# Transposing the softmax of a group of queries one group later

## The chip, the cores and the metric

The kernel runs on one core of one Trainium2 chip. The metric is the device time of one execution in microseconds (us). Before the change it is 2257.52 us in the median of three runs (2251.76 to 2259.87).

The engines are named as in the profile: PE is TensorE (matrix products, transposes), PEld its loading of weights, DVE is VectorE, ACT is ScalarE, POOL is GpSimd, SP is the engine that issues nearly all DMAs.

## The reference

One layer mixes three branches over 2048 positions of width 1024: a gated short convolution, a Fourier mix, and attention over a neighbourhood. What matters here is the attention. Positions form a grid of 32 rows by 64 columns. A block of 16 query columns in one row looks at 8 rows of keys in a window of 32 columns, with a learned bias and a mask, and also at 256 context keys. One softmax goes over both:

```python
s_loc = jnp.einsum('bnqhd,binchd->bhnqic', qr, kb).astype(jnp.float32) * scale + bias
s_loc = jnp.where(mask, s_loc, NEG_INF)
s_ctx = jnp.einsum('bnqhd,bkhd->bhnqk', qr, k_ctx).astype(jnp.float32) * scale
sc = jnp.concatenate([s_loc.reshape(b, h, n_cb, Q_BLOCK_W, n_loc), s_ctx], axis=-1)
p = jax.nn.softmax(sc, axis=-1).astype(v.dtype)
```

The weights p are then applied to the values of the window and of the context. Before this come a normalization and one wide projection of the input to all branches; after it a projection per branch, sigmoid gates, an output projection and a last normalization.

## The kernel before

The wide projection is done in pairs of output tiles, with a scheme of seven products for each pair. A product is twelve matmuls of 128x512 (lines 310 to 312) into one of three banks (mm). After each of its seven products a pair calls a background hook.

In the second half of the projection the hook (line 1141) advances a generator, `both`, by 2.7 steps a call on the average. It yields first the steps of `attention`, then those of `fourier`, then some preparations of the tail. So the program text is a sequence of products with a few attention steps after each. The framework then orders the instructions of each engine when the program is built: the place in the text is the priority, and an instruction whose operands or buffers it holds to be late lets others go ahead. On the chip each engine works off its list in that order.

Attention goes over 32 units (4 pairs of heads, 4 blocks of columns, 2 heads of the pair), and in each unit over 4 groups of 128 queries, 128 groups in all. Each group has these steps:

- scores (`scores`): the bias is loaded (line 823). Four matmuls give the context scores sx and the window scores sl (lines 883 to 886). VectorE takes the maxima and writes the biased scores into a tile P (lines 890, 891), ScalarE exponentiates (lines 893, 894), VectorE adds up, inverts and normalizes P (lines 895 to 897). P has three buffers, sl one bank, sx two.
- turn (`do_turn`, `turn`): P is transposed in five or six pieces (line 931), three at a time into one bank (tr); each batch is copied to a tile PT (line 941), the first by VectorE, the second by ScalarE. PT has four buffers, two for each group. The first turn of a block of columns also loads its values vt (line 912), which have one buffer.
- weigh: after every second turn the transposed weights of two groups are multiplied with the values (line 953, bank po), the result is copied by ScalarE (line 954), and after two such steps stored (line 957).

With the scores of the last group of a unit, `prepare_qk` loads queries and keys of the next one. The keys are split into KH by ScalarE (line 131) and KL by GpSimd (line 132); KH and KL have one buffer each, T, the scaled queries, two.

A turn isn't taken right after its scores: it is put into a list, `turns`, and taken from it one group later, after that group's scores. Likewise the weigh that a turn makes due goes into a list, `weighs`, and is taken after the next scores. So in a unit the steps are: scores and turn for the first and third group, and scores, weigh and turn for the second and fourth.

Of the kernel before, what the change touches and what calls it, by code (L numbers as in the profile page):

```python
# [59 lines left out]
def emit(tc, I, out, dbg=None):  # L60
# [776 lines left out]
    def attention():  # L837
# [4 lines left out]
        def keys_ctx(pr):  # L842
            r = []
            for hd in range(2):
                raw = at.tile([128, 512], F32, tag="raw", name="rawc", bufs=3)
                dup_load(raw[:, :CT], kcd[pr][hd * 64 : hd * 64 + 64, :])
                a = at.tile([128, CT], F32R, tag="kch", name="kch", bufs=2)
                b_ = at.tile([128, CT], F32R, tag="kcl", name="kcl", bufs=2)
                split(a, b_, raw[:, :CT], nc.scalar, nc.gpsimd)
                r.append((a, b_))  # L850
            return r
# [19 lines left out]
        def scores(head, ct, g, qk, kc, bt):  # L871

            T, KH, KL = qk
            w = KW[ct]
            n = G_NR[g] * w
            if g != 2:
                bt = at.tile([128, 480], F32, tag="bt", name="bt", bufs=2)
                bias_load(head, CTYPE[ct], g, n, w, bt)
            sl = pat.tile([128, 512], F32, tag="sl", name="sl")
            sx = pat.tile([128, CT], F32, tag="sx", name="sx", bufs=2)  # L880
            tq = T[:, g * 128 : g * 128 + 128]
            ks = slice(G_R0[g] * w, G_R0[g] * w + n)
            nc.tensor.matmul(sx, tq, kc[0], start=True, stop=False)
            nc.tensor.matmul(sx, tq, kc[1], start=False, stop=True)
            nc.tensor.matmul(sl[:, :n], tq, KH[:, ks], start=True, stop=False)
            nc.tensor.matmul(sl[:, :n], tq, KL[:, ks], start=False, stop=True)
            P = at.tile([128, CT + 480], F32, tag="P", name="P", bufs=3)
            Pl = P[:, CT : CT + n]
            sm = smt()
            nc.vector.tensor_reduce(sm[:, 0:1], sx, AX.X, ALU.max)  # L890
            nc.vector.tensor_tensor_reduce(Pl, sl[:, :n], bt[:, :n], 1.0, sm[:, 0:1], ALU.add, ALU.max, accum_out=sm[:, 1:2])
            nc.vector.tensor_scalar(sm[:, 2:3], sm[:, 1:2], -1.0, None, ALU.mult)
            nc.scalar.activation(P[:, :CT], sx, AF.Exp, bias=sm[:, 2:3], accum_out=sm[:, 3:4])
            nc.scalar.activation(Pl, Pl, AF.Exp, bias=sm[:, 2:3], accum_out=sm[:, 4:5])
            nc.vector.tensor_scalar(sm[:, 5:6], sm[:, 3:4], sm[:, 4:5], 2.0, ALU.add, ALU.mult)
            nc.vector.reciprocal(sm[:, 6:7], sm[:, 5:6])
            nc.vector.tensor_scalar(P[:, : CT + n], P[:, : CT + n], sm[:, 6:7], None, ALU.mult)
            return P, bt
# [5 lines left out]
        def values(pr, ct):  # L904
            vt = at.tile([128, 9, 128], F32, tag="vt", name="vt")
            c0, w = KCS[ct], KW[ct]
            pieces = ((0, 0, 4, 8),) if w == 32 else ((1, 4, 5, 3), (4, 12, 5, 4), (0, 0, 4, 1), (8, 20, 2, 1))
            for first, row, rows, cnt in pieces:
                for r in range(rows):
                    base = vd[pr][(row + r) * 64 + c0 : (row + r) * 64 + c0 + w, :]  # L910
                    src = AP(tensor=base.tensor, offset=base.offset, ap=[[128, w], [rows * 64 * 128, cnt], [1, 128]])
                    load(vt[r * w : r * w + w, first : first + cnt, :], src)
            return vt

        def turn(head, ct, g, P, vt):

            p0 = head % 2 * 64
            w = KW[ct]
            n = G_NR[g] * w
            ch = [(P[:, x * 128 : x * 128 + 128], 128, vc[x][:, head * 64 : head * 64 + 64]) for x in range(2)]  # L920
            at_ = 0
            for piece_, rows in (MID if w == 32 else EDGE)[g]:
                e = min(at_ + 128, n)
                ch.append((P[:, CT + at_ : CT + e], e - at_, vt[: rows * w, piece_, p0 : p0 + 64]))
                at_ += rows * w
            lst = []
            for c0 in range(0, len(ch), 3):
                grp = ch[c0 : c0 + 3]
                pt = pat.tile([128, 512], F32, tag="tr", name="tr")
                for x, (src, w_, _) in enumerate(grp):  # L930
                    nc.tensor.transpose(pt[:w_, x * 128 : x * 128 + 128], src, ident)  # L931
                PT = at.tile([128, 384], F32, tag="PT", name="PT", bufs=PTB)
                eng = nc.vector if c0 == 0 else nc.scalar
                x = 0
                while x < len(grp):
                    y = x
                    while y < len(grp) and grp[y][1] == grp[x][1]:
                        y += 1
                    w_ = grp[x][1]
                    d_, s_ = PT[:w_, x * 128 : y * 128], pt[:w_, x * 128 : y * 128]  # L940
                    eng.copy(d_, s_) if eng is nc.scalar else eng.tensor_copy(d_, s_)  # L941
                    x = y
                for x, (_, _, v_) in enumerate(grp):
                    lst.append((v_, PT[: v_.shape[0], x * 128 : x * 128 + 128]))
            return lst

        def weigh(pr, ct, hd, gp, pts, ost):
            po = pat.tile([128, 128], F32, tag="po", name="po")
            for x in range(max(len(l) for l in pts)):
                for z in range(2):  # L950
                    if x < len(pts[z]):
                        v_, p_ = pts[z][x]
                        nc.tensor.matmul(po[z * 64 : z * 64 + 64, :], v_, p_, start=x == 0, stop=x == len(pts[z]) - 1)
            nc.scalar.copy(ost[:, gp, :], po)
            if gp == 1:
                for z in range(2):
                    store(od[pr][hd * 64 : hd * 64 + 64, z::2, ct, :], ost[z * 64 : z * 64 + 64])

        turns, weighs = [], []
        V = {}  # L960

        def do_turn(pr, ct, hd, g, P):
            if (pr, ct) not in V:
                V[pr, ct] = values(pr, ct)
            lst = turn(2 * pr + hd, ct, g, P, V[pr, ct])
            if g % 2 == 0:
                V["half"] = lst
                if g == 0:
                    V["ost"] = at.tile([128, 2, 128], F32, tag="ost", name="ost")
            else:  # L970
                weighs.append((pr, ct, hd, g // 2, [V["half"], lst], V["ost"]))
# [4 lines left out]
        for i, (pr, ct, hd) in enumerate(groups):  # L976
            bt = None
            for g in range(4):
                P, bt = scores(2 * pr + hd, ct, g, qk, kc[hd], bt)
                if g == 3 and i + 1 < len(groups):  # L980
                    if groups[i + 1][0] != pr:
                        kc = keys_ctx(groups[i + 1][0])
                    qk = prepare_qk(*groups[i + 1])
                yield
                if weighs:
                    weigh(*weighs.pop())
                    yield
                if turns:
                    do_turn(*turns.pop())
                    yield  # L990
                turns.append((pr, ct, hd, g, P))
        do_turn(*turns.pop())
        yield
        weigh(*weighs.pop())
        yield
        et.close()

    def fourier():
# [133 lines left out]
    def both():  # L1132
        yield from attention()
        vcs.close()
        yield from fourier()
        yield from tail_pools()
# [229 lines left out]
```

## Time and profile before

| | us |
|---|---|
| median of three runs | 2257.52 |
| lowest and highest | 2251.76, 2259.87 |
| the profiled execution | 2256.13 |
| its span, from first to last instruction | 2254.4 |
| PE busy | 2132.9 |
| DVE busy | 1547.0 |
| ACT busy | 887.1 |
| POOL busy | 1011.5 |

The profile is of one execution. An engine is busy while one of its instructions runs; the matmuls are pipelined, so that a busy PE needn't be a PE at its peak. Idle time is put down to what ended it. Attention lies between about 915 and 1570 us of the span. Lines are those of the kernel; lines 131, 132 and 310 to 312 belong to helpers that many places use, and the names of the tiles tell these apart.

### The profile page before, as it was taken

What the parts mean: (1) busy time and instruction counts of PE and PEld (TensorE: products, weight loads), DVE (VectorE), ACT (ScalarE), POOL (GpSimd) and SP (SyncE); (2) the same over time, 40 slices, a digit from 0 to 9 for tenths busy, and PEclk for the clock granted to TensorE, in tenths of its full rate; (3) what the DMA queues carried; (4) which work ended last, traced back from release to release, by engine and by line L of the source; (5) the groups of instructions that cost most, each with busy time, mean ns of one, the idle gap of its engine ahead of it and who ended that gap; (6) DMA issues with size and microseconds to landing.
All of it is one profiled execution on the core that took longest, in us unless ns stands there. A gap on an engine that the chain in (4) does not pass through costs nothing. (4 is left out here: it accounts for less than half of the span.)

```text
span 2254.4 us, 32033 instructions
## 1 busy us (share of the span) xinstructions
PE 2132.9 (95%) x10588; PEld 1686.6 (75%) x10588; DVE 1547.0 (69%) x2731; ACT 887.1 (39%) x2011; POOL 1011.5 (45%) x761
## 2 busy tenths in 40 slices
PE   6899989999999899999999999999999898999998
PEld 4678768888788687777777777777757677878777
DVE  6864685565665665778787788786736868787773
ACT  3443222334544442454555555554213332222121
POOL 2753467654464654444444334343415243434341
PEclk8999999999999899999999999999999999999999
DMA  6244644233233344343444444453466676666561
GB/s 255 80 136 117 225 174 168 94 108 117 94 101 111 101 142 131 109 126 107 142 127 127 139 148 127 141 149 127 154 211 218 212 223 214 192 206 191 173 190 67
DMA packets 198863, 336.78 MB, mean 149 GB/s; under 512 B 22249, under 2 KB 89129, under 8 KB 197546
## 3 DMA queue, kind: packets, MB, share of 16 engines
q1 hardware_dynamic: 198554, 334.47, 46.8%
q8 instruction: 84, 1.38, 0.3%
q14 instruction: 81, 0.66, 0.1%
q10 hardware_dynamic: 144, 0.26, 0.0%
HBM read 248.27 MB, written 86.38 MB: 148 GB/s over the span
## 5 line engine op out<-in xcount | busy, mean ns | idle before, releaser
L131 ACT CAST wh<-wr 128x512 fp32r<-128x512 f32 x384 | 237.7, 620 | 479.1 <-PE mm L311 388.1
L132 DVE TENSOR_TENSOR wl<-wr,wh 128x512 fp32r<-128x512 f32 x256 | 244.7, 957 | 37.0 <-ACT wh L131 36.8
L132 POOL TENSOR_TENSOR wl<-wr,wh 128x512 fp32r<-128x512 f32 x128 | 173.7, 1360 | 212.8 <-ACT wh L131 191.0
L337 POOL TENSOR_TENSOR ws<-wr 128x512 f32<-128x512 f32 x62 | 89.0, 1435 | 309.0 <-DMA wr<-w_in 255.3
L395 DVE SCALAR_TENSOR_TENSOR st<-mm,bin,tp 128x512 f32<-128x512 f32 x158 | 118.0, 747 | 143.0 <-PE mm L312 136.0
L132 POOL TENSOR_TENSOR wbl<-wr,wbh 128x512 fp32r<-128x512 f32 x96 | 130.9, 1367 | 163.0 <-ACT wbh L131 160.4
L126 PE MATMUL mm<-yh,wbh 128*128 128x512 f32 x384 | 153.5, 400 | 17.8 <-DVE tg L1238 10.4
L128 PE MATMUL mm<-yh,wbl 128*128 128x512 f32 x384 | 152.8, 398 | 2.3 <-POOL wbl L132 2.3
L127 PE MATMUL mm<-yl,wbh 128*128 128x512 f32 x384 | 151.8, 396 | 0.3 <-DVE yl L132 0.3
L931 PE MATMUL tr<-ident,P 128*128 128x128 f32 (+3 forms) x672 | 120.4, 280 | 19.1 <-DVE PT L941 7.9
L132 POOL TENSOR_TENSOR wl<-ws,wh 128x512 fp32r<-128x512 f32 x62 | 83.7, 1350 | 112.5 <-ACT wh L131 94.8
L931 PEld LDWEIGHTS tr<-ident,P 128*128 128x128 f32 (+3 forms) x672 | 78.9, 139 | 68.4 <-DVE PT L941 25.4
L355 POOL TENSOR_TENSOR wr<-wr 128x512 f32<-128x512 f32 x64 | 87.9, 1373 | 93.7 <-DVE wl L132 58.8
L450 DVE TENSOR_TENSOR st<-mm,tp 128x512 f32<-128x512 f32 x96 | 65.9, 686 | 87.2 <-PE mm L312 84.4
L310 PE MATMUL mm<-B11h,wh 128*128 128x512 f32 x256 | 104.5, 408 | 14.0 <-DVE tp L353 7.4
L131 ACT CAST wbh<-wr 128x512 fp32r<-128x512 f32 x96 | 59.2, 620 | 127.6 <-PE mm L127 61.0
L126 PE MATMUL po<-wo,mh 128*128 128x512 f32 x256 | 101.2, 395 | 7.8 <-DVE xn L1261 7.7
L310 PE MATMUL mm<-T4h,wh 128*128 128x512 f32 x256 | 103.1, 403 | 4.5 <-DVE tp L345 4.5
L311 PE MATMUL mm<-B11l,wh 128*128 128x512 f32 x256 | 103.0, 402 | 4.2 <-DVE B11l L132 4.2
L339 POOL TENSOR_TENSOR wr<-ws,wr 128x512 f32<-128x512 f32 x62 | 84.3, 1360 | 49.6 <-DVE wl L132 36.3
L310 PE MATMUL mm<-B21h,wh 128*128 128x512 f32 x256 | 102.6, 401 | 3.6 <-DVE st L450 2.8
L310 PE MATMUL mm<-T2h,wh 128*128 128x512 f32 x256 | 102.8, 402 | 1.4 <-ACT T2h L131 1.4
(319 smaller groups left out, 6293.3 us busy)
## 6 DMA issues: line engine op xcount, KB each, us to landing
wr<-w_in SPq DMA_DIRECT2D x136, 512.0 KB
gd<-st SPq DMA_DIRECT2D x96, 256.0 KB
wr<-w_br SPq DMA_DIRECT2D x96, 256.0 KB
tg<-gd SPq DMA_DIRECT2D x96, 256.0 KB
tab<-dft SPq DMA_DIRECT2D x40, 256.0 KB
wa<-w_ada SPq DMA_DIRECT2D x32, 256.0 KB
rawq<-qd SPq DMA_DIRECT2D x64, 128.0 KB
rawk<-kd SPq DMA_DIRECT2D x64, 128.0 KB
```

The lines of the kernel that those rows point to most:

```text
L126: nc.tensor.matmul(ps, ah, bh, start=first, stop=False)
L127: nc.tensor.matmul(ps, ah, bl, start=False, stop=False)
L128: nc.tensor.matmul(ps, al, bh, start=False, stop=last)
L131: heng.copy(hi, src) if heng is nc.scalar else heng.tensor_copy(hi, src)
L132: return leng.tensor_tensor(lo, src, hi.bitcast(F32), ALU.subtract)
L310: nc.tensor.matmul(ps, w[0][:, s], oh, start=first and k == 0, stop=False)
L311: nc.tensor.matmul(ps, w[0][:, s], ol, start=False, stop=False)
L337: ptt(t1, a21, a22, ALU.add)
L339: ptt(a11, t1, a11, ALU.subtract)
L355: ptt(a12, a12, a11, ALU.subtract)
L395: stt(dst, ps, bc(m), add, ALU.add, ALU.add)
L931: nc.tensor.transpose(pt[:w_, x * 128 : x * 128 + 128], src, ident)
```

## The change

The list `turns` now holds two groups: after the scores of a group the turn of the group two before it is taken, the oldest first, where it was the turn of the group before. The weigh still follows the turn that makes it due by one group, so it moves with it. At the end two turns are left, and each is followed by a weigh if one is due.

```diff
                 if weighs:
                     weigh(*weighs.pop())
                     yield
-                if turns:
-                    do_turn(*turns.pop())
+                if len(turns) > 1:
+                    do_turn(*turns.pop(0))
                     yield
                 turns.append((pr, ct, hd, g, P))
-        do_turn(*turns.pop())
-        yield
-        weigh(*weighs.pop())
-        yield
+        while turns:
+            do_turn(*turns.pop(0))
+            yield
+            if weighs:
+                weigh(*weighs.pop())
+                yield
         et.close()
```

Buffers, instructions and their number stay as they are. In a unit the steps become: scores, weigh and turn for the first and third group, scores and turn for the second and fourth.

## Rows read from the trace of the kernel before

**Rows 1.** The page: busy us, share of the span and instructions of each engine.

```profile
PE 2132.9 (95%) x10588; PEld 1686.6 (75%) x10588; DVE 1547.0 (69%) x2731; ACT 887.1 (39%) x2011; POOL 1011.5 (45%) x761
```

**Rows 2.** Busy time by stretch: length, five engines, granted clock, DMA share, GB/s.

```profile
915.00:1570.00 655.00, 633.42 (x3998) 484.93 (x3998) 517.67 (x1300) 349.78 (x1069) 270.79 (x207) 1.00 0.44 129
1570.00:2254.00 684.00, 641.75 (x2751) 501.22 (x2749) 460.23 (x662) 181.03 (x322) 255.92 (x198) 0.98 0.58 189
```

**Rows 3.** Waits of PE, 915 to 1570 us: us in total, times, longest.

```profile
PE tr L931 <- DVE PT L941: 7.9, 19, 1.2
PE tr L931 <- DVE P L897: 7.9, 10, 2.3
PE sl L886 <- POOL KL L132: 2.4, 2, 1.3
PE tr L931 <- DVE sm L896: 1.1, 1, 1.1
PE tr L931 <- DVE sm L892: 1.1, 2, 0.9
PE tr L931 <- DVE sm L895: 0.4, 1, 0.4
```

**Rows 4.** In order of time, one change of unit: start, duration, engine, line, operation.

```profile
1110.79 0.36 PE L883 MATMUL sx<-kch,T 128*128 128x256 f32 x1
...
1113.27 2.51 POOL L132 TENSOR_TENSOR KL<-rawk,KH 128x512 fp32r<-128x512 f32 x2
...
1117.41 0.50 DVE L897 TENSOR_SCALAR P<-P,sm 128x544 f32<-128x544 f32 x1
...
1117.47 0.37 PE L883 MATMUL sx<-kch,T 128*128 128x256 f32 x1
...
1121.46 0.49 PE L931 MATMUL tr<-ident,P 128*128 128x128 f32 x3
...
1121.71 0.36 PE L883 MATMUL sx<-kch,T 128*128 128x256 f32 x1
```

**Rows 5.** Waits of PE's weight loads, 915 to 1570 us.

```profile
PEld tr L931 <- DVE PT L941: 25.4, 66, 1.6
...
PEld tr L931 <- DVE P L897: 6.3, 5, 2.8
```

**Rows 6.** In order of time: last and first scores around two changes of unit.

```profile
929.67 0.28 PE L883 MATMUL sx<-kch,T 128*128 128x256 f32 x1
...
937.06 0.28 PE L883 MATMUL sx<-kch,T 128*128 128x256 f32 x1
...
1535.78 0.28 PE L883 MATMUL sx<-kch,T 128*128 128x256 f32 x1
...
1540.06 0.36 PE L883 MATMUL sx<-kch,T 128*128 128x256 f32 x1
```

**Rows 7.** The chain in order of time: one weigh (start, us, what).

```profile
1546.45 1.75 PE po L953 x20
```

**Rows 8.** In order of time: VectorE's writes of P beside transposes, two places.

```profile
950.14 0.52 DVE L891 CUSTOM_DVE_ANT_0 P<-sl,bt,sm 128x288 f32<-128x288 f32 x1 [0.20 <-PE sl L886]
...
950.40 0.38 PE L931 MATMUL tr<-ident,P 128*128 128x128 f32 x2
...
1532.36 0.44 PE L931 MATMUL tr<-ident,P 128*128 128x128 f32 x2
...
1532.78 0.59 DVE L891 CUSTOM_DVE_ANT_0 P<-sl,bt,sm 128x360 f32<-128x360 f32 x1
```

**Rows 9.** Waits of SP's queue, 915 to 1570 us.

```profile
SPq L912 <- PE po L953: 17.5, 10, 2.6
```

**Rows 10.** In order of time, the end of attention.

```profile
1561.98 0.47 PE L310 MATMUL mm<-B11h,wh 128*128 128x512 f32 x1
...
1563.30 0.54 PE L953 MATMUL po<-PT,vc 128*64 128x128 f32 x5
```

## The prediction

> **What bounds the kernel now.** I read the page's busy times first [rows 1]: TensorE is busy 95% of the span, the next engine, VectorE, 69%. Then the same by stretch [rows 2]: attention runs as background work from about 915 to 1570 us. In these 655.0 us TensorE is busy 633.4 us, so it idles 21.6 us; VectorE is busy 517.7 us, so it idles 137.3 us. The granted clock there is 1.00, so no clock is to be won or lost. A change to the order of the steps of attention that adds and removes no instruction can change only such idle time. Then the waits of TensorE in this stretch [rows 3]. The reader is to see that nearly all of them stand before the transposes of line 931, and that they are of two kinds: the one bank for transposed tiles is still being copied out (PT, 7.9 us in 19 waits), or the softmax is not yet normalized (P, 7.9 us in 10 waits; sm, which is VectorE still at the small steps of a softmax, 1.1 + 1.1 + 0.4 us in 4). The second kind is 10.5 us together. No matmul of the projection products (mm) is in the list.
>
> Last, single places in order of time. One shows where the planner really puts things [rows 4]. The scores of one group start at 1110.79, its softmax is normalized from 1117.41 to 1117.91, and its transposes start at 1121.46. Between them stand the scores of the next group (1117.47); those of the one after it start at 1121.71. So a softmax takes 7.1 us from its scores to its end, longer than the 6.7 and 4.2 us from one group's scores to the next, and the transposes, one group late in the program, run on the chip almost two groups late already, just ahead of the scores of the second group after.
>
> **The change, part by part.** I write S(n) for the scores and softmax of group n, T(n) for its transposes and their copies, W for the values of two groups. Counts stay: 128 S, 128 T, 64 W, 320 steps, so what follows attention starts at the same place between the products, and only waits are to be summed.
>
> *T(n) moves from between S(n+1) and S(n+2) to between S(n+2) and S(n+3).* What goes is the wait for the softmax, 10.5 us [rows 3]. On the chip T(n) already ran next to S(n+2), so I expect it to move behind S(n+2): which makes it later by the four matmuls of these scores, and by more wherever a product lies between. The waits were 0.75 us in the mean (10.5 us over 14) and 2.3 us at most, so I let all but parts of the longest go and take 9 us; below stands 0 (the planner lets the new place slide until it is as tight again), above the 10.5 us, and with the weight loads that waited for P while a matmul still drained (6.3 us in 5 [rows 5]) 16.8 us. Here the Trainium skill speaks ("Perfetto Trace Analysis", section "Identifying the Most-Contended Engine"): matmul busy time flatters a pipelined engine, and the busy share of weight loads shows the headroom better. The trace agrees that the two differ: in this stretch weight loads are busy 484.9 of 655.0 us, 74%, against 97%. Read by that rule the gain would be the 16.8 us and not 9; I keep the matmul rows, since a weight load that waits while a matmul drains costs nothing until the array is empty.
>
> *What is late next: the copy out of the bank.* A turn's second transposes need VectorE's copy of the first and the one bank. That wait (7.9 us) stays as it is, since the copies and their bank are untouched. Bounds: all 7.9 us could go if VectorE's order happens to become kinder; it could double. I take 0, no reason for either sign.
>
> *W moves by one group too, and leaves the place behind the loading of new keys.* Before, the steps between the last scores of a unit S(3) and the first of the next unit S(0') were W and T; after, T alone. S(0') needs KL, and KH and KL have one buffer each: S(3) must have read them, then ScalarE casts, then GpSimd subtracts. At the place shown GpSimd ends at 1115.78, 5.0 us after S(3) started [rows 4]. From S(3) to S(0') it is 7.39 us at the first of 31 such places and 4.28 us at the last [rows 6], in the mean over the 31 about 6.4 us. Without W, whose 20 matmuls take 1.75 us [rows 7], S(0') comes due at or before the end of KL nearly everywhere. The planner then puts products, W or T ahead of it, so the price is only where GpSimd is later than planned. Today that happens 2 times of 31, 2.4 us together [rows 3]. Ends: 0, and 31 times 1.2 us = 37 us. Transposes, which were planned that tightly for P, waited 14 times of 128, which would be 3.4 of 31; I take 5 times 1.2 us, since four instructions on two engines stand in this chain: 6.0 - 2.4 = +3.6 us.
>
> *P is held one group longer, with three buffers.* VectorE's first write of P (line 891) of group n+3 needs T(n) to be over, and T(n) now stands directly ahead of S(n+3). I laid the change onto the trace of before: in the place of each T stands that of one group earlier, and the write that would then need it is that of the next but one group of today. In 33 of 126 places the write starts before those transposes end: first at 950.14 against 950.78, last at 1532.78 against 1532.80 [rows 8]; the 33 come to 18.2 us, on VectorE. Behind a waiting write stand VectorE's copies of PT and the evacuations of products, and TensorE waits for those. Ends: 0 (VectorE does something else of its 137.3 idle us) and 18.2 us (all passed on). Today TensorE waits for no evacuation here, so I stay near the low end: +2 us. Here the skill speaks against the change ("Perfetto Trace Analysis", section "Optimization Strategy"): the same gap again and again on the engine that should be full can mean that there is no buffer for the next tile. The row of the copies agrees with it, 19 waits for one bank; for P no row of before shows it. By that rule the end would be the 18.2 us, the rival below.
>
> *SP's queue.* With T goes the loading of the values (line 912), with W the store of the result (line 957), each by one group; bias loads, keys and weights of the products stand in the same queue. The loading still stands two groups ahead of its use. No wait of TensorE's matmuls in the stretch is for a DMA [rows 3], the products hide it: 0. If that cover went, SP's own waits at line 912, 17.5 us in 10 [rows 9], are the upper bound; nothing argues for a gain.
>
> *The end.* Two T and two W are left instead of one each, and T(126) needs two of the four PT buffers that only the W behind it frees. Products follow on TensorE there (line 310 at 1561.98, between the last group's transposes and its values [rows 10]), so 0; without them at most a W and the transposes, some 3 us once (1.75 us for a W, and five transposes with their copies).
>
> Sum: -9 + 0 + 3.6 + 2 + 0 + 0 = -3.4 us. The profiled execution took 2256.1 us (span 2254.4 and 1.7 around it), 1.4 us under the median of the three runs, 2257.5, which themselves lie 8 us apart. 2256.1 - 3.4 = 2252.7; I say 2252.5.
>
> **The rivals.**
> *More goes than P.* Transposes that are ready when they are due let the planner and VectorE's copies fall better, and the waits for the bank go with the others: all 18.4 us of idle time before line 931 on TensorE, 2237.7 us. For it: weight loads wait 25.4 us in 66 for the bank [rows 5], the largest loss of the stretch, so small shifts count. Against it: bank and copy are unchanged. Chance 0.20.
> *It does nothing on the chip.* The planner already ran T next to S(n+2); only two neighbours swap, and new chance waits replace the old: 2256 within 3 us. Chance 0.14.
> *KL takes the place of P (slower).* At each of the 31 changes of unit S(0') is planned right at the end of KL and TensorE stands for the 1.2 us that it stood in the two cases: 37 - 2.4 - 9 = +25.6, 2281.7 us. It makes the kernel slower than before from 10 such waits on (12 - 2.4 - 9 = +0.6) and by over 0.5% from 19. For it: one buffer, and W is gone from between. Against: 29 of 31 got through, and the planner has products to put there. Chance 0.12.
> *P's buffers (slower or even).* All 18.2 us of late writes reach TensorE: 18.2 - 9 = +9.2, 2265.3 us. For it: three buffers for a life of nearly three groups. Against: VectorE is idle a fifth of the stretch. Chance 0.09.
> My forecast has 0.45.
>
> **How the numbers follow.** A measurement of this kernel tells from no change about 0.5%, 11.3 us. Of my forecast, which I give a range of 2243 to 2261, 0.10 lies below 2246.2, 0.34 within and 0.01 above 2268.8. Of the larger gain 0.18 is faster and 0.02 within; the second rival is all within; of KL 0.11 is slower and 0.01 within; of the buffers 0.03 slower and 0.06 within. Faster 0.28, within 0.57, slower 0.15. The range reaches to the larger gain's price below and just past the buffers' price above, and leaves out most of the KL case: 2237 to 2269.
>
> **What would show it.** In the waits of TensorE from 915 to 1570 us, P and sm before line 931 fall from 10.5 to about 1.5 us; PT stays near 8; sl for KL rises to some 6. VectorE's write at line 891, which no transposes hold up now, begins to wait for them. Attention ends some 3 us earlier, and the stretch after it, 684 us [rows 2], is as long as before. It is wrong if P waits stay, if KL or line 891 dominate, or if the time comes or goes after 1570 us.

## The result and the profile after

The changed kernel takes 2267.1 us (median of 5 runs, 2265.9 to 2269.7), the kernel before 2257.2 on the same chip: ratio 1.0053, 95% interval 1.0035 to 1.0072 (the ratio is that of the means, 2267.7 and 2255.7; that of the medians is 1.0044). It is 9.9 us slower by the medians; 2252.5 us had been forecast. The page's first part, as [rows 1]:

```profile
span 2263.8 us, 31970 instructions
...
PE 2138.4 (94%) x10588; PEld 1690.8 (75%) x10588; DVE 1543.0 (68%) x2731; ACT 887.3 (39%) x2011; POOL 1009.0 (45%) x761
```

By stretch, as [rows 2], the columns the same:

```profile
0.00:915.00 915.00, 859.81 (x3854) 702.68 (x3855) 570.54 (x773) 356.54 (x622) 484.99 (x357) 0.98 0.41 135
915.00:1570.00 655.00, 626.24 (x3925) 478.56 (x3923) 512.46 (x1293) 346.08 (x1057) 269.34 (x203) 0.99 0.43 128
1570.00:2264.00 694.00, 652.40 (x2813) 509.51 (x2811) 460.02 (x665) 184.72 (x332) 254.63 (x201) 0.98 0.58 187
```

In the attention stretch TensorE idles 28.8 us, where it idled 21.6, and gets fewer instructions done. The last instructions of line 953 show where the time is lost; first the kernel before, then the one after (the numbers around "to" are the first and the last start):

```profile
L953 PE MATMUL po<-PT,vt x832: 269/273/324, 930.8 to 1564.6; 128*64 128x128 f32 x68, 120*64 120x128 f32 x60, 96*64 96x128 f32 x29, 48*64 48x128 f32 x10
```

```profile
L953 PE MATMUL po<-PT,vt x832: 269/273/421, 929.7 to 1575.6; 128*64 128x128 f32 x68, 120*64 120x128 f32 x60, 96*64 96x128 f32 x29, 48*64 48x128 f32 x10
```

Attention ends 11.0 us later. From its first scores (920.9 before, 918.4 after) to its last weigh it takes 657.5 us and not 644.0, with the same 1421 product matmuls in between. What follows it is 1.6 us shorter. So all of the loss is in attention. The waits of TensorE there, as [rows 3]:

```profile
PE sl L886 <- POOL KL L132: 9.5, 7, 3.5
PE tr L931 <- DVE PT L941: 9.2, 18, 1.3
PE sl L885 <- DVE sm L891: 4.8, 5, 1.6
PE tr L931 <- DVE sm L892: 2.6, 2, 2.2
PE sx L883 <- DVE T L859: 1.6, 2, 0.9
PE tr L931 <- ACT PT L941: 0.7, 1, 0.7
```

Of the kernel before, one line of this list is not in [rows 3]:

```profile
PE sl L885 <- DVE sm L891: 0.2, 1, 0.2
```

The reader is to see an exchange. The waits for the softmax have gone from 10.5 to 2.6 us, none of them for P itself. In their place stand waits at the change of unit: for KL (2.4 before), for the bank sl, which holds the scores of the last group until line 891 has read them (0.2 before), and for the scaled queries T (0 before). They come to 15.9 us, where it was 2.6. All of them stand before the first scores of a new unit, but for one: of the 9.5 us for KL, 6.0 us in 6 waits stand there, and the longest, 3.5 us, before the second scores of a unit. The whole list is 28.4 us, 7.4 more than the 21.0 of before. On VectorE line 891 now waits for transposes, which it did nowhere before:

```profile
DVE P L891 <- PE tr L931: 8.9, 14, 3.6
```

The place of [rows 4], in order of time:

```profile
1109.79 0.28 PE L883 MATMUL sx<-kch,T 128*128 128x256 f32 x1
...
1110.54 0.36 PE L883 MATMUL sx<-kch,T 128*128 128x256 f32 x1
...
1110.75 1.14 ACT L131 CAST KH<-rawk 128x512 fp32r<-128x512 f32 x2
...
1111.70 2.52 POOL L132 TENSOR_TENSOR KL<-rawk,KH 128x512 fp32r<-128x512 f32 x2
...
1113.04 0.43 PE L886 MATMUL sl<-KL,T 128*128 128x352 f32 x1 [0.50 <-POOL KL L132]
1113.52 0.59 DVE L891 CUSTOM_DVE_ANT_0 P<-sl,bt,sm 128x352 f32<-128x352 f32 x1 [1.35 <-PE sl L886]
```

The scores of the new unit now start 0.75 us behind the last of the old (6.7 us in [rows 4]); over the 31 changes of unit it is 3.5 us in the mean, where it was 6.4. TensorE then waits for the keys, and VectorE behind it for TensorE.

A long wait can cost more than itself. The longest ends at 1405.26:

```profile
1400.04 1.27 POOL L337 TENSOR_TENSOR ws<-wr 128x512 f32<-128x512 f32 x1 [4.15 <-DMA wr<-w_in]
...
1404.03 1.17 POOL L132 TENSOR_TENSOR KL<-rawk,KH 128x384 fp32r<-128x384 f32 x1
...
1405.26 0.43 PE L886 MATMUL sl<-KL,T 128*128 128x360 f32 x1 [3.46 <-POOL KL L132]
...
1406.06 0.63 PE L310 MATMUL mm<-B22h,wh 128*128 128x512 f32 x1
1406.49 0.63 PE L311 MATMUL mm<-B22l,wh 128*128 128x512 f32 x1
1406.92 0.63 PE L312 MATMUL mm<-B22h,wl 128*128 128x512 f32 x1
...
1409.40 0.40 PE L311 MATMUL mm<-B22l,wh 128*128 128x512 f32 x1
1409.63 0.40 PE L312 MATMUL mm<-B22h,wl 128*128 128x512 f32 x1
```

This is the wait before the second scores of a unit, the first unit of a new pair of heads. They need the second half of the keys, which GpSimd begins only at 1404.03, behind three operations for the products (lines 337 to 339, from 1400.04 on). The product matmuls behind the wait start 0.43 us apart, until at 1409.40 they are back at 0.23. That is TensorE at 1.2 GHz, the lower of its two levels, for some 3 us, and at 2.4 before and after; the granted clock of the stretch says the same:

```profile
1405.00:1410.00 5.00, 4.74 (x16) 3.73 (x17) 1.07 (x4) 0.55 (x3) 0.21 (x1) 0.66 0.53 146
```

I estimate the cost of such a drop from this row as (1 - 0.66) x 5 = 1.7 us. By stretches of 5 us the kernel before has one in attention, just behind its wait of 1.30 us for KL at 1439.81:

```profile
1440.00:1445.00 5.00, 5.00 (x18) 3.96 (x18) 3.19 (x8) 1.02 (x5) 3.83 (x4) 0.66 0.62 177
```

The changed kernel has three: this one, one behind a wait of 2.2 us at 1453.6, one behind a wait of 1.6 us for KL at 1486.0. That is some 3.4 us more. So of the 13.5 us that attention is longer, 7.4 are waits and some 3.4 clock; the remaining 2.7 I have not traced.

### The profile page after: what moved, and what is told of

Same layout as the page of the kernel before. It is cut to its first block, busy times and chain, and to the rows that moved or that the text cites. A ratio compares the mean times of both kernels' runs of the same rounds, so it can differ in the third digit from the quotient of the medians.

```text
span 2263.8 us, 31970 instructions
## 1 busy us (share of the span) xinstructions
PE 2138.4 (94%) x10588; PEld 1690.8 (75%) x10588; DVE 1543.0 (68%) x2731; ACT 887.3 (39%) x2011; POOL 1009.0 (45%) x761
## 5 line engine op out<-in xcount | busy, mean ns | idle before, releaser
L132 DVE TENSOR_TENSOR wl<-wr,wh 128x512 fp32r<-128x512 f32 x256 | 246.2, 963 | 38.7 <-ACT wh L131 38.6
L337 POOL TENSOR_TENSOR ws<-wr 128x512 f32<-128x512 f32 x62 | 88.1, 1421 | 321.9 <-DMA wr<-w_in 246.1
L126 PE MATMUL mm<-yh,wbh 128*128 128x512 f32 x384 | 153.9, 401 | 18.4 <-DVE tg L1240 10.5
L931 PE MATMUL tr<-ident,P 128*128 128x128 f32 (+3 forms) x672 | 121.0, 281 | 12.8 <-DVE PT L941 9.2
L931 PEld LDWEIGHTS tr<-ident,P 128*128 128x128 f32 (+3 forms) x672 | 79.6, 139 | 58.0 <-DVE PT L941 24.7
L310 PE MATMUL mm<-B22h,wh 128*128 128x512 f32 x256 | 103.1, 403 | 1.8 <-DVE tp L341 1.8
```

The costliest lines, as they stand in the source:

```text
L126: nc.tensor.matmul(ps, ah, bh, start=first, stop=False)
L132: return leng.tensor_tensor(lo, src, hi.bitcast(F32), ALU.subtract)
L310: nc.tensor.matmul(ps, w[0][:, s], oh, start=first and k == 0, stop=False)
L337: ptt(t1, a21, a22, ALU.add)
```

## The experiments

Three theories. U: the loss lies at the change of unit, because W no longer stands between the loading of the new keys and the scores that need them. P: the three buffers of P, held longer, cost it. N: any other order of the attention steps moves the time by some 10 us, and this is no more.

To compare orders I worked out from the list in order of time, for each matmul of attention, how much later than usual it starts after the one before it (usual is 0.23 us behind 512 columns, in proportion for less, 0.11 behind a transpose or a weigh). "Loss at tr" is the sum before transposes, "at sl" before lines 885 and 886. "Weigh" is TensorE's busy time at line 953. With every delay counted, however short, the column at tr comes out 3 to 7 us higher in all kernels alike, so only differences between its rows are read. The ratio is to the kernel before on the same chip, whose median there was 2252.7 us for the w0, kv and g0 kernels, 2254.8 for the x kernels, 2256.1 at 2.6 and 2.8; so compare ratios, and medians only within a family.

| kernel | median us | ratio (95%) | attention us | loss at tr | loss at sl | weigh |
|---|---|---|---|---|---|---|
| before | 2257.2 | 1 | 644.0 | 30.2 | 5.5 | 120.1 |
| after | 2267.1 | 1.0053 (1.0035 to 1.0072) | 657.5 | 24.6 | 20.8 | 122.5 |
| b_w0 | 2280.5 | 1.0124 (1.0107 to 1.0141) | 667.8 | 33.4 | 8.7 | 129.5 |
| a_w0 | 2266.3 | 1.0053 (1.0038 to 1.0069) | 659.0 | 24.1 | 9.1 | 131.8 |
| a_kv | 2257.2 | 1.0016 (1.0002 to 1.0029) | 649.0 | 28.7 | 11.4 | 122.6 |
| b_kv | 2250.6 | 0.9991 (0.9980 to 1.0002) | 637.3 | 26.8 | 2.9 | 120.6 |
| b_x | 2271.9 | 1.0081 (1.0059 to 1.0102) | 655.5 | 43.0 | 3.2 | 120.6 |
| a_x | 2266.3 | 1.0050 (1.0034 to 1.0066) | 658.2 | 24.1 | 16.9 | 122.8 |
| a_xp4 | 2267.7 | 1.0053 (1.0032 to 1.0074) | 652.4 | 24.7 | 13.3 | 122.8 |
| a_xw1 | 2268.7 | 1.0060 (1.0038 to 1.0083) | 653.2 | 42.8 | 8.0 | 116.2 |
| b_r26 | 2275.6 | 1.0088 (1.0073 to 1.0104) | 674.4 | 47.2 | 4.3 | 120.8 |
| a_r26 | 2264.5 | 1.0034 (1.0020 to 1.0048) | 667.8 | 26.9 | 19.2 | 118.8 |
| b_r28 | 2277.6 | 1.0092 (1.0077 to 1.0107) | 639.5 | 38.7 | 3.0 | 120.6 |
| a_r28 | 2270.6 | 1.0052 (1.0034 to 1.0071) | 634.0 | 22.1 | 15.4 | 120.5 |
| a_g0 | 2265.8 | 1.0061 (1.0039 to 1.0083) | 658.7 | 27.3 | 8.1 | 129.5 |
| a_g0t | 2261.7 | 1.0034 (1.0022 to 1.0046) | 653.9 | 29.5 | 7.6 | 130.0 |
| a_g0kv | 2263.4 | 1.0045 (1.0030 to 1.0061) | 654.7 | 24.9 | 6.9 | 133.3 |
| a_g0tkv | 2257.4 | 1.0023 (1.0009 to 1.0037) | 648.8 | 22.4 | 8.4 | 129.9 |

Attention, losses and weigh are those of the one profiled execution, which can lie off the median (in a_x by 14 us above). At 2.6 and 2.8 attention spans more and fewer products, so its length is compared within a pair.

**W moved alone (b_w0), and W moved back (a_w0).** On the kernel before; on the changed kernel the same two steps change places.

```diff
-                if weighs:
-                    weigh(*weighs.pop())
-                    yield
                 if turns:
                     do_turn(*turns.pop())
                     yield
+                if weighs:
+                    weigh(*weighs.pop())
+                    yield
```

> The kernel before with one edit: the weigh W is taken directly behind the turn that makes it due, not after the next scores. So W alone moves to the groups where the changed kernel has it (first and third of a unit), while the transposes T stay one group late. Theory U (the change costs time because W no longer stands between the loading of new keys and the first scores of the new unit): scores to scores across the change of unit falls from 6.4 us to about 3.5, the waits of TensorE for KL, for the bank sl and for T there rise from 2.6 us to some 15, the 10.5 us of waits for the softmax stay: about 2257 + 13 = 2270 us. Theory P (the three buffers of P, held longer because T is later, cost the time): T is not later here, 2257 within 4 us. A W right behind its T may wait for its copies, by up to some us in either theory.

> The changed kernel with the same edit: T two groups late, W directly behind the turn that makes it due, which puts W back to the second and fourth group of a unit, behind the loading of new keys, as in the kernel before. Theory U: scores to scores across the change of unit back to about 6 us, the waits for KL, sl and T there back to about 3 us, the waits for the softmax gone as in the changed kernel: 2257 - 8 = 2249 us. Theory P: T is as late as in the changed kernel and P is held as long, so 2267 us as there, with line 891 waiting for transposes some 9 us.

Both results miss theory U's times, and b_w0, 28 us slower, misses P's as well. A weigh right behind its turn has a price of its own: the same 1344 matmuls of line 953 keep TensorE busy 129.5 and 131.8 us, where 120.1 and 122.5 had done. Apart from that the loss at sl in a_w0 is 9.1 us and not 20.8, as U says. P's time came out in a_w0, but not for P's reason: line 891 waits for transposes only 1.8 us there. In b_w0 theory U fails in its mechanism too: the waits for KL, sl and T come to 4.4 us and not 15, the loss at sl rises by 3.2 us only, and scores to scores across the change are 4.3 us. There the step left in between is a turn that still waits for its softmax (such waits rose to 17.3 us). So W's leaving alone doesn't make the cost at sl; it seems to take ready transposes as well, which no run tests by itself. The experiment was not clean.

**The chain of the keys shortened (a_kv), with its control (b_kv).**

```diff
-                split(KH[:, s], KL[:, s], raw[:, :m], nc.scalar, nc.gpsimd)
+                split(KH[:, s], KL[:, s], raw[:, :m], nc.scalar, nc.gpsimd if x else nc.vector)
```

> The changed kernel with the first half of each KL subtracted by VectorE in place of GpSimd (0.7 to 0.95 us for 1.3, 32 times, some 27 us more for VectorE). Theory U: the wait for KL, 9.5 us in the changed kernel, falls to 2 or 3 us; the waits for the bank sl stay: 2267 - 6 = 2261 us. Theory P: the keys are not the cause, VectorE is fuller: 2267 to 2272 us.

> Control: the kernel before with the same edit, first half of KL on VectorE. Its waits for KL are 2.4 us, so theory U gives 2255 to 2259 us; theory P the same, 2257 and up to 5 us more for the fuller VectorE.

The changed kernel gains 0.37% (1.0053 to 1.0016), some 8 us; the kernel before 0.09%, within its interval nothing. The waits of a_kv:

```profile
PE tr L931 <- DVE PT L941: 15.0, 22, 1.9
PE sl L885 <- DVE sm L891: 4.4, 8, 0.9
PE tr L931 <- DVE sm L892: 2.0, 2, 1.4
PE sl L886 <- DVE KL L132: 1.0, 2, 0.8
```

KL is gone from the top, no wait is over 2 us, and no stretch of 5 us in attention has a lower clock. The bank sl still costs 4.4 us. Against its control a_kv is still slower, by 1.0016 / 0.9991 = 1.0025, 6.6 us in the medians, where without this edit the change costs 0.53%. So about half of the loss came by way of the keys. Theory P expected no gain here, and there is one.

**Four buffers for P (a_xp4), W one group later (a_xw1), and their controls.** To make room the split weights of the products got three buffers (b_x on the kernel before, a_x on the changed one):

```diff
-        wh = wp.tile([128, 512], F32R, tag="wh", name="wh" + nm, bufs=4)
-        wl = wp.tile([128, 512], F32R, tag="wl", name="wl" + nm, bufs=4)
+        wh = wp.tile([128, 512], F32R, tag="wh", name="wh" + nm, bufs=3)
+        wl = wp.tile([128, 512], F32R, tag="wl", name="wl" + nm, bufs=3)
```

a_xp4 is a_x with

```diff
-            P = at.tile([128, CT + 480], F32, tag="P", name="P", bufs=3)
+            P = at.tile([128, CT + 480], F32, tag="P", name="P", bufs=4)
```

and a_xw1 is a_x with six PT buffers (PTB = 6) and

```diff
-                if weighs:
-                    weigh(*weighs.pop())
+                V["n"] = 4 * i + g
+                if weighs and weighs[0][0] < V["n"] - 1:
+                    weigh(*weighs.pop(0)[1:])
                     yield
...
-                weighs.append((pr, ct, hd, g // 2, [V["half"], lst], V["ost"]))
+                weighs.append((V["n"], pr, ct, hd, g // 2, [V["half"], lst], V["ost"]))
...
```

(the two places of the list `weighs` are shown out of order; the last `weigh`, behind the loop, changes likewise).

> Control for the next three: the kernel before with three buffers in place of four for the split weights of the products (wh, wl), which frees 4 KB of each partition. Both theories: a small loss or none, 0 to +6 us on the kernel before.

> Control: the changed kernel with the same three buffers for wh and wl. Both theories: 8 to 16 us slower than the control of the kernel before, as the changed kernel is than the kernel before, with sl waiting for KL some 9 us.

> The changed kernel with three buffers for wh and wl and four for P. Theory P (late writes of P at line 891 hold the bank sl and with it TensorE): line 891 no longer waits for transposes (8.9 us in the changed kernel), sl no longer waits for line 891 (4.8 us): 8 us or more faster than its control. Theory U (new keys are late because S of the new unit comes too early): the wait for KL stays at some 9 us; 0 to 5 us faster than its control. From the run with KL on VectorE I expect U to hold the larger part: 4 us faster.

> The changed kernel with three buffers for wh and wl, six for PT, and W taken one group later still, two after its last turn. So W is back behind the loading of new keys without standing right behind its turn, whose copies it then waited for (the matmuls of line 953 cost about 13 us more in both kernels that had that). Theory U: scores to scores across the change of unit back to about 6 us, the wait for KL back to 2 to 4 us, 8 to 12 us faster than its control and even with the control of the kernel before. Theory P: P is held as in the changed kernel: within 3 us of its control, sl waiting for line 891 some 5 us.

The controls brought the surprise. With one weight buffer less the kernel before loses 0.81%, the changed kernel nothing, and the changed one is now the faster: 1.0050 / 1.0081 = 0.997, though narrowly, since the two intervals overlap. The traces can't show where: the profiled execution of a_x is its slowest, 7 us longer than that of b_x. The loss at tr of b_x is 43.0 us, 12.8 more than that of the kernel before, and its loss at sl as small as there. Four buffers for P gain nothing (1.0053 against 1.0050, where theory P wanted 8 us, 0.35%), though no write at line 891 waits for transposes any more: theory P is refuted as the main cause. W back in its place brings the scores across the change of unit back to 6.1 us and the loss at sl to 8.0, as U says; but the loss at tr, chiefly for the bank (25.5 us of waits for PT), eats it up, and the 8 to 12 us that U expected did not come.

**Other orders for both kernels: 2.6 and 2.8 steps a call (b_r26, a_r26, b_r28, a_r28).** This asks theory N directly.

```diff
-        pair(*p, bg=lambda: bgr(dbg.get("rate", 2.7)))
+        pair(*p, bg=lambda: bgr(dbg.get("rate", 2.6)))
```

(2.8 likewise.)

> The kernel before with 2.6 steps of background work a call in place of 2.7: the same work, the attention steps a little thinner between the products. It gives the planner another order and serves as a control for the changed kernel at the same rate. All theories: within 0.5% of the kernel before; waits for the softmax near 10 us, sl waits under 4 us.

> The changed kernel at 2.6 steps a call. Theory U (scores of a new unit come too early for the keys and the bank sl): waits of TensorE before the sl matmuls at 8 to 15 us as at 2.7, so 6 to 13 us slower than the kernel before at 2.6. Theory N (every change of order moves the time by some us either way, and the 10 us are that): between 10 us faster and 10 us slower than its control, sl waits between 2 and 15 us.

> The kernel before with 2.8 steps a call. All theories: within 0.5% of the kernel before; waits for the softmax 10 us or more, since the scores lie closer together, sl waits under 4 us.

> The changed kernel at 2.8 steps a call. Theory U: sl waits 8 to 18 us, 6 to 15 us slower than the kernel before at 2.8. Theory N: between 10 us faster and 10 us slower than its control.

The kernel before is 0.9% slower at both neighbours of its rate, outside what all theories allowed. The changed kernel stays at 0.3 to 0.5% over the kernel before at 2.7, whatever the rate, so at 2.6 and 2.8 the change makes the kernel faster: 1.0034 / 1.0088 = 0.9946, 1.0052 / 1.0092 = 0.9960. The waits at 2.6, first without, then with the change:

```profile
PE tr L931 <- DVE PT L941: 16.8, 21, 1.7
PE tr L931 <- DVE P L897: 6.4, 8, 1.3
PE tr L931 <- DVE sm L892: 5.2, 4, 3.5
PE tr L931 <- DVE sm L895: 2.5, 4, 1.0
PE tr L931 <- DVE sm L896: 1.2, 1, 1.2
PE sl L885 <- DVE sm L891: 1.2, 1, 1.2
```

```profile
PE tr L931 <- DVE PT L941: 12.4, 22, 1.6
PE sl L886 <- POOL KL L132: 7.3, 8, 2.4
PE sl L885 <- DVE sm L891: 4.7, 7, 1.4
PE tr L931 <- DVE sm L892: 2.5, 2, 1.4
```

The two columns of losses in the table say it for four pairs (own order, x, 2.6, 2.8). At sl the change costs about the same in each: +15.3, +13.7, +14.9, +12.4 us. At tr it gives back 5.6, 18.9, 20.3, 16.6 us. The kernel before in its own order has a small loss at tr, 30.2 us, where b_x, b_r28 and b_r26 have 39 to 47. There are two pairs more. With half of KL on VectorE (kv) the loss at tr is as small without the change, 26.8 us, the change gives nothing back there (+1.9) and costs 8.5 us at sl: it is slower. With W right behind its turn (w0) it costs 0.4 us at sl and gives back 9.3 at tr: it is faster, 1.0053 / 1.0124 = 0.993. So the change is slower in two of six pairs, the two in which the loss at tr was smallest without it.

These losses are not the whole difference. In the profiled executions the changed kernel's attention is 6.6 us shorter at 2.6 and 5.5 us at 2.8, but 9.3 and 4.3 us are gained behind attention, and at 2.8 4.5 us are lost ahead of it; with three weight buffers attention is 2.7 us longer. Theory N is right about the sign of the result, which hangs on the order, theory U about the cost at sl.

**One step turned back at each change of unit (a_g0, a_g0t), alone and with a_kv's edit (a_g0kv, a_g0tkv).** Ahead of the scores in the loop over the groups of the changed kernel (the last two added lines in a_g0t and a_g0tkv only):

```diff
+                if g == 0 and weighs:
+                    weigh(*weighs.pop())
+                    yield
+                    do_turn(*turns.pop(0))
+                    yield
                 P, bt = scores(2 * pr + hd, ct, g, qk, kc[hd], bt)
```

> The changed kernel with one step turned round at each change of unit: in the first group of a unit W stands ahead of the scores, not behind. So there is W again between the loading of new keys and the scores that need them. Theory U (scores of a new unit come too early): scores to scores across the change of unit from 3.5 us to 5 or 6, the loss before sl matmuls (20.8 us in the changed kernel, 5.5 in the kernel before, by the starts of the matmuls) to 5 to 9 us; against it W stands right behind a turn in half the cases, 5 to 7 us: 3 to 8 us faster than the changed kernel, some 2260 us. Theory N (any other order is 10 to 20 us slower than the one order of the kernel before, whatever is in it): 2264 to 2277 us.

> The same, and the next turn also ahead of the scores of the new unit: S(3), T(1), W, T(2), S(0'). Theory U: sl loss down to that of the kernel before, 3 to 6 us, scores to scores across the change over 6 us; T(2) comes earlier, so some waits for the softmax return, 2 to 5 us: 2255 to 2262 us. Theory N: 2264 to 2277 us.

> W ahead of the scores of a new unit and the first half of KL on VectorE. Both remedies aim at the same wait, so theory U expects little more than the better of the two alone: 2252 to 2260 us. Theory N: 2264 to 2277 us.

> W and the next turn ahead of the scores of a new unit and the first half of KL on VectorE: sl loss as small as in the kernel before with that edit (2.9 us), softmax waits fewer than there. Theory U: 2245 to 2255 us, even with or a little better than the kernel before. Theory N: 2264 to 2277 us.

Scores to scores across the change go to 6.1 us (a_g0) and 8.1 us (a_g0t), the loss at sl from 20.8 to 8.1 and 7.6 us, the waits for KL from 9.5 to 2.1 and 2.4: moving that one step is enough to regain most of the cost at sl, as theory U says. In a_g0t, where the one wait left for KL is again before the second scores of a unit, at 1405.78:

```profile
PE tr L931 <- DVE PT L941: 15.9, 22, 1.4
PE sl L886 <- POOL KL L132: 2.4, 1, 2.4
PE tr L931 <- DVE sm L892: 1.9, 4, 0.7
PE tr L931 <- DVE P L897: 0.9, 2, 0.7
PE sl L885 <- DVE sm L891: 0.6, 2, 0.5
```

But the weigh right behind its turn takes back 7 to 8 us (129.5 and 130.0 us at line 953), and the bank for transposes some more, so a_g0 gains nothing and a_g0t 0.19%. a_g0tkv, which had been expected at 2245 to 2255 us, is at 1.0023, no better than a_kv. Laid on the 2257.2 us of the first chip, the four ratios give 2271, 2265, 2267 and 2262 us: all miss U's ranges, and three lie in N's. No version beat the kernel before clearly; b_kv, at 0.9991 with 1 within its interval, is as fast.

## Why the prediction was wrong

- *What goes with the later T, -9 us:* right in kind and nearly in size. The waits for the softmax fell by 7.9 us, from 10.5 to 2.6, those for P to none; the loss at tr fell by 5.6 us.
- *The copy out of the bank, 0:* right here (7.9 to 9.2 us). In other orders it moves between 5 and 25 us, by far the largest scatter, and I had seen no reason for either sign.
- *W leaves the place behind the loading of new keys, +3.6 us:* this is the step that failed: the term was mis-sized by what it left out. I priced only the wait of the first scores for KL, and that came out: 6 of the 31 changes of unit waited, 6.0 us together, where I had 5 times 1.2. But scores that stand so close behind the last ones wait for whatever comes late there: for the bank sl (0.2 to 4.8 us), for T (0 to 1.6), and once, before the second scores, for the second half of the keys (3.5). All waits at the change of unit rose by 13.3 us (2.6 to 15.9) and not by 3.6, more than the waits for the softmax gave back; by the starts of the matmuls the loss at sl rose by 15.3. I took too much comfort from the rule that the planner would put products ahead of late scores. Where an engine takes longer on the chip, TensorE, which works off its list in order, stands: ahead of the wait of 1.6 us for sl at 990.37 VectorE normalizes 736 columns in 1.60 us (from 988.17), where the same in the kernel before takes 0.59 at 1128.55. That the planner had reckoned with the shorter time is my reading; no run shows its durations.
- *The clock:* I said that none was to be won or lost. The 1.00 of [rows 2] is a rounded mean, which hides one stretch at 1.2 GHz. Behind long waits at KL and at a softmax the changed kernel has three: some 3.4 us more.
- *P's buffers, +2 us:* line 891 did begin to wait for transposes, 8.9 us in 14 times. With four buffers these waits went and the time did not change, so of the 18.2 us that I had laid on the trace no price shows. None of the five waits for the bank sl stands behind such a wait; VectorE was at other work ahead of line 891. The Trainium skill's rule on consistent bubbles ("Perfetto Trace Analysis", section "Optimization Strategy") speaks of gaps on the engine that should be saturated. Those for P stood on VectorE, busy 78% of this stretch, so the rule didn't bear on them.
- *SP's queue and the end, 0:* nothing in the traces speaks against it.
- *The rivals:* "KL takes the place of P", at 0.12, had the sign, but neither the price (2281.7 us) nor the way: its 31 waits for KL were 6. "P's buffers", at 0.09, came nearest with 2265.3 us, by luck, since its mechanism is the one that a_xp4 refutes; so it is luck, too, that the time lies within the outer 2237 to 2269. What no rival said is that the sign hangs on the order that the kernel before happens to have. At 2.6, at 2.8 and with fewer weight buffers the forecast's sign holds, with 11, 7 and 6 us gained in the medians, though only part of that lies in attention, and in the traces of the x pair none; with half of KL on VectorE it doesn't, 6.6 us lost.

Open is why the order at 2.7 steps a call is so kind to the transposes, why the time behind attention changes with it, and how much of a new order's scatter comes from durations that the planner misjudges; no run here takes that apart. Nor do the runs show that the loss at sl alone makes up the 9.9 us: the edits that take it away again (a_w0, a_xw1, a_g0) add losses elsewhere, and the one that gains time (a_kv) regains about half against its control.

## What to carry to other kernels

When steps of an order move, ask for each gap that closes what the step behind it needs, not only for the gap that opens: here 8 us of waits went at one place, and 13 us came at another. A change of order is a sample of one from orders that scatter by 10 us or more; measure both versions under two or three neighbouring settings before the change itself is credited or blamed. And a shorter chain at the point that has become tight (the first half of KL on VectorE) gave back more here than moving the steps again.

## What the runs showed of the hardware

- TensorE fell to 1.2 GHz for some 3 us behind waits of 1.3 to 3.5 us, with shorter gaps around them, on an engine that was otherwise busy: in the kernel before behind 1439.81, in the changed kernel behind 1405.26, 1453.6 and 1486.0. Not every such wait was followed by a drop: none came behind the wait of 2.3 us at 956.9 in the kernel before, nor behind that of 2.4 us at 1405.78 in a_g0t. In a_kv, where no wait was over 2 us, there is no drop in attention. Each costs some 1.7 us beyond the wait, an estimate from the granted 0.66 of 5 us.
- The matmuls of a weigh alternate between two halves of the output's partitions. Where half or all of the weighs were issued right behind their turns (w0 and g0 kernels), the same 1344 matmuls kept TensorE busy 129 to 133 us and not 116 to 123. That the operands of one half were then late, and that the two halves no longer ran beside each other, is my reading of it, not shown by a run of its own.
